# A float32 trunk on split operands: 2x2 block chains without subtracted copies, w_down one block later, left operands made one by one behind weight splits

## The chip, the cores and the metric

One core of a Trainium2 chip runs the whole program. The metric is the time of one execution on the device, in microseconds (us), as the median of three runs. The engines work side by side, each through its own queue in order: TensorE (PE in the rows, PEld its weight loads), VectorE (DVE), ScalarE (ACT), GpSimd (POOL) and SyncE (SP), which issues the loads of weights. An instruction at the head of a queue that waits holds everything behind it.

## The reference

256 positions of width 2048 go through two residual layers, each followed by a SwiGLU layer. The even layer has SSD heads and MLA heads side by side, the odd one stick-breaking attention.

```python
def reference(x, mix_norm, ffn_norm, w_in, ..., w_gate, w_up, w_down, final_norm):
    cos, sin = rope_tables(x.shape[1], x.dtype)
    for layer in range(DEPTH):                       # DEPTH = 2
        h = rms_norm(x, mix_norm[layer])
        if layer % 2 == 0:
            mix = ssd_mla_mixer(h, w_in[e], ..., w_out_even[e], cos, sin)   # concat(y_ssd, y_mla) @ w_out
        else:
            mix = stick_breaking_mixer(h, w_qkv[o], w_out_odd[o])           # heads @ w_out
        x = x + mix
        x = x + swiglu_ffn(rms_norm(x, ffn_norm[layer]), w_gate[layer], w_up[layer], w_down[layer])
    return rms_norm(x, final_norm)

def swiglu_ffn(h, w_gate, w_up, w_down):
    return (jax.nn.silu(h @ w_gate) * (h @ w_up)) @ w_down
```

D_MODEL is 2048, the hidden width of the SwiGLU layer 5632 (11 blocks of 512), everything is float32.

## The kernel before

**Split operands.** Every float32 operand of a matmul is split into a high and a low half: ACT casts it to the high half (L268), DVE subtracts that from the operand to get the low half (L269). A product is then three matmuls: high by high, low by high, high by low. Left operands are transposed on TensorE so that the contraction lies on the partitions.

**A pair.** `pair` multiplies the 256 rows by two blocks of 512 columns of weights at a time (w_gate and w_up of one hidden block; two blocks of an out-projection). Its contraction of 2048 falls in four blocks of 512. Blocks 0 and 1 are done as a 2x2 block product with seven multiplications in place of eight, M1 to M7, whose left operands are seven sums of quarters of x (`st["S"]`) and whose right operands are the weight blocks b11, b12, b21, b22 and four differences of them (t1, t2, b12 in place, M4's). Blocks 2 and 3 are done plainly as c0 to c3, two tiles each. So a pair has 15 products of 12 matmuls (128x512), 11 splits of weights and four weight differences (L526, `wsub`). Raw weights lie in a ring of four 1 MB tiles, high and low halves in rings of three each, differences in a ring of two.

**Banks.** A pair accumulates in four PSUM banks, z, p2, p3 and p4. In the kernel before M1, M5, M6 and M7 all go to z, and after each of them ACT copies the bank out (L612). DVE twice subtracts an earlier copy (L615), so that what is left can be added to the other banks; z itself, when complete, needs no copy. The order of the products is the tuple `MIXED`, or `LATE` in the second half of an out-projection of MLA and of the stick-breaking layer.

**Operands of a pair.** `operand_block` transposes one block of the left side. When the second of blocks 0 and 1 is there, `operand_ready` makes the four sums and seven splits in one go; with `wait` over 1 (15 from `norm_operand`), under a pressing priority and not before the last copy of a product (`self.kept`).

**Order of the work.** TensorE's order is written by hand: tasks (generators for transposes, attention heads and so on) are woken at `tick()`, at most two at a time, between the matmuls of the big products. On the other engines a scheduler sets the order by priority: weight work counts up from 100000 (`wprio`), work under `urgent()` has 50000, anything else 10000000. `issue_after` forbids an instruction to come ahead of another one.

**SwiGLU layer.** Groups of 2, 2, 2, 2 and 3 pairs; after each group the transposed activations of the group are multiplied by the group's rows of w_down, four column blocks one after another, each added to the residual (`xres`, L425).

Other lines that the rows name: L278 transposes a block of x and L289 to L290 make its halves; L304 and L1120 copy transposed tiles out of PSUM; L444 adds a copy of a product to a bank; L474, L497 and L498 make the operand sums of `operand_ready`; L769 is the stick-breaking output product; L1135 and L1159 are the scores and the output of an MLA head, L1155 is the ACT copy ahead of the latter; L361 to L363 are the matmuls of `project` (w_in, w_qkv, w_down), L559 those of `pair`.

## Time and profile before

| | before |
| --- | --- |
| time, median of 3 runs | 2460.2 us (2457.3 to 2462.13) |
| the profiled execution's own time | 2460.24 us |
| its span, first to last instruction | 2458.5 us |
| TensorE busy | 2419.7 us, 98% |
| DVE busy | 1837.9 us, 75% |
| ACT busy | 1344.2 us, 55% |
| chain that ended last, by engine | PE 88%, DVE 7%, issue 2%, ACT 1%, DMA 1% |
| mean granted clock of TensorE | 0.996 |

TensorE is busy for nearly all of the span, and the chain followed back from the end runs over it for 88%. The time is in two parts, then: what TensorE has to do, and the few stretches in which it isn't at work or has a low clock. Those stretches are found by cutting the span in pieces of 50 us, and read in the timelines of the engine that is waited for.

### The profile page before, as it was taken

The page shows a single profiled execution, that of the slowest core. Times are in us where ns is not written, and L with a number is a line of the kernel's source. Part 1 is how long each engine was busy: PE and PEld are TensorE (multiplying, and loading weights), DVE is VectorE, ACT ScalarE, POOL GpSimd, SP SyncE. Part 2 cuts the span into 40 slices and gives each one's busy share as a digit, 9 for nine tenths or more (in the row PEclk, how much of TensorE's full clock was granted, in tenths as well). Part 3 has the DMA queues.
Part 4 walks back from the last instruction along what each step waited for, and adds up shares of the span by engine and source line. Part 5 has one row for each costly group of instructions (what it writes and reads, how often), then busy time and mean ns, then how long its engine had stood idle before and what let it go on. Part 6 is the DMA issues. An engine that isn't in the chain of part 4 may idle for free.

```text
span 2458.5 us, 27627 instructions
## 1 busy us (share of the span) xinstructions
PE 2419.7 (98%) x11104; PEld 1991.0 (81%) x11104; DVE 1837.9 (75%) x1561; ACT 1344.2 (55%) x1337; POOL 136.9 (6%) x165
## 2 busy tenths in 40 slices
PE   8999999999999999999999999999999999999998
PEld 7888888777788888888888888878788888888887
DVE  5876596578988878787975446469988888787975
ACT  6665564455654555454554556656654545454563
POOL 1341101110000000000000000000000000000001
PEclk9999999999999999999999999999999999999999
DMA  8564556424555556565655555545556656565653
GB/s 273 174 204 154 171 189 187 126 98 138 202 208 187 203 179 218 171 234 175 223 189 189 173 171 169 173 137 177 192 196 201 201 185 203 180 229 171 240 193 115
DMA packets 257824, 454.77 MB, mean 185 GB/s; under 512 B 20716, under 2 KB 45424, under 8 KB 257696
## 3 DMA queue, kind: packets, MB, share of 16 engines
q1 hardware_dynamic: 255168, 446.48, 54.3%
q0 software_dynamic: 1952, 5.48, 0.7%
q8 instruction: 87, 1.43, 0.2%
q10 hardware_dynamic: 576, 1.05, 0.1%
q14 instruction: 41, 0.34, 0.0%
HBM read 450.85 MB, written 2.13 MB: 184 GB/s over the span
## 4 chain that ended last, share of the span: by engine, by line
PE 88%; DVE 7%; issue 2%; ACT 1%; DMA 1%; SPq 0%; ACTq 0%; DVEq 0%
PE acc L559 39%; PE acc L361 14%; PE acc L363 14%; PE acc L362 14%; DVE wl L269 4%; PE tr L278 1%; DVE wsum L526 1%; ACT wh L268 1%; PE at L1060 1%; PE at L1136 1%; PE tr L302 0%; DVE w L526 0%; DVE s L269 0%; PE at L1135 0%; DVE s L444 0%
## 5 line engine op out<-in xcount | busy, mean ns | idle before, releaser
L269 DVE TENSOR_TENSOR wl<-w,wh 128x2048 fp32r<-128x2048 f32 (+2 forms) x431 | 967.9, 2256 | 391.3 <-ACT wh L268 387.9
L268 ACT CAST wh<-w 128x2048 fp32r<-128x2048 f32 (+2 forms) x431 | 804.7, 1876 | 537.2 <-PE acc L363 312.7
L559 PE MATMUL acc<-wh,s 128*128 128x512 f32 x3360 | 842.7, 392 | 5.8 <-DVE s L269 2.4
L559 PEld LDWEIGHTS acc<-wh,s 128*128 128x128 f32 x3360 | 628.1, 188 | 137.0 <-ACT s L612 3.6
L361 PE MATMUL acc<-wh,s 128*128 128x512 f32 (+1 forms) x1600 | 637.7, 399 | 0.6 <-ACT wh L268 0.6
L363 PE MATMUL acc<-wh,s 128*128 128x512 f32 (+1 forms) x1600 | 622.1, 389 | 0.0
L362 PE MATMUL acc<-wl,s 128*128 128x512 f32 (+1 forms) x1600 | 620.8, 388 | 0.2 <-DVE wl L269 0.2
L559 PE MATMUL acc<-wl,s 128*128 128x512 f32 x1680 | 453.0, 391 | 6.2 <-DVE wl L269 6.0
L559 PEld LDWEIGHTS acc<-wl,s 128*128 128x128 f32 x1680 | 314.6, 188 | 77.9 <-DVE wl L269 12.9
L363 PEld LDWEIGHTS acc<-wh,s 128*128 128x128 f32 x1600 | 301.0, 188 | 63.4
L362 PEld LDWEIGHTS acc<-wl,s 128*128 128x128 f32 x1600 | 301.8, 189 | 58.0 <-issue 1.2
L361 PEld LDWEIGHTS acc<-wh,s 128*128 128x128 f32 x1600 | 301.7, 189 | 57.7 <-issue 1.2
L269 DVE TENSOR_TENSOR wl<-wsum,wh 128x2048 fp32r<-128x2048 f32 x84 | 192.0, 2297 | 15.1 <-ACT wh L268 15.0
L268 ACT CAST wh<-wsum 128x2048 fp32r<-128x2048 f32 x84 | 160.9, 1915 | 69.1 <-PE acc L559 33.6
L526 DVE TENSOR_TENSOR wsum<-w,wsum 128x2048 f32<-128x2048 f32 x56 | 128.6, 2297 | 9.9 <-DMA w<-in_w_up_dram 7.9
L612 ACT COPY s<-acc 128x512 f32<-128x512 f32 x112 | 65.7, 586 | 103.8 <-PE acc L559 103.8
L629 ACT ACTIVATE s<-s,rstd 128x512 f32<-128x512 f32 x44 | 31.9, 725 | 103.6 <-DVE s L628 103.6
L773 POOL TENSOR_SCALAR_AFFINE_SELECT s<-s 128x256 f32<-128x256 f32 x16 | 15.7, 980 | 1112.2 <-ACT s L772 1112.2
L526 DVE TENSOR_TENSOR wsum<-w,w 128x2048 f32<-128x2048 f32 x28 | 64.7, 2312 | 8.2 <-DMA w<-in_w_up_dram 5.6
L526 DVE TENSOR_TENSOR w<-w,w 128x2048 f32<-128x2048 f32 x28 | 64.4, 2299 | 0.0
L425 DVE TENSOR_TENSOR xres<-acc,xres 128x512 f32<-128x512 f32 x76 | 51.4, 689 | 10.9 <-PE acc L363 10.3
L316 ACT ACTIVATE s<-acc,rstd 128x512 f32<-128x512 f32 x48 | 32.1, 687 | 45.3 <-PE acc L363 44.0
(230 smaller groups left out, 1277.5 us busy)
## 6 DMA issues: line engine op xcount, KB each, us to landing
w<-in_w_gate_dram SPq DMA_DIRECT2D x88, 1024.0 KB, 5.1
w<-in_w_up_dram SPq DMA_DIRECT2D x88, 1024.0 KB, 5.1
w<-in_w_down_dram SPq DMA_DIRECT2D x88, 1024.0 KB, 5.1
w<-in_w_qkv_dram SPq DMA_DIRECT2D x48, 1024.0 KB, 5.1
w<-in_w_in_dram SPq DMA_DIRECT2D x47, 1024.0 KB, 5.1
w<-in_w_out_even_dram SPq DMA_DIRECT2D x32, 1024.0 KB, 5.0
w<-in_w_out_odd_dram SPq DMA_DIRECT2D x16, 1024.0 KB, 4.9
w<-in_w_ukv_dram SPq DMA_DIRECT2D x32, 256.0 KB, 4.2
```

Of the source, the lines that this page charges most:

```text
L268: nc.scalar.copy(hi, src)
L269: nc.vector.tensor_tensor(lo, src, hi.bitcast(F32), op=ALU.subtract)
L278: self.nc.tensor.transpose(pt[:, k, t * P:(t + 1) * P], src(t, 2 * k2 + k), self.ident)
L316: self.nc.scalar.activation(o, ps[t], func, scale=scale[:, t:t + 1])
L361: nc.tensor.matmul(ps[t], hi[:, ts], wh, start=k == 0, stop=False)
L362: nc.tensor.matmul(ps[t], hi[:, ts], wl, start=False, stop=False)
L363: nc.tensor.matmul(ps[t], lo[:, ts], wh, start=False, stop=k == nk - 1)
L425: nc.vector.tensor_tensor(xs, c, xs, op=ALU.add)
L526: self.nc.vector.tensor_tensor(o, p, q, op=ALU.subtract)
L559: nc.tensor.matmul(ps[b], x, y, start=b not in started, stop=stop, skip_group_check=True)
L612: self.kept = [nc.scalar.copy(o, ps["z"]).ins]
L629: nc.scalar.activation(s, s, AF.Silu, scale=rstd[:, t:t + 1])
```

## The change

1. The banks are dealt out anew: M1, M6 and M7 go to z, M5 and M3 to p3, M2 to p2, M4 to p4. The two subtractions of copies (L615) of a pair go, and z, which now has no M5 in it, gets one more addition of a copy. Four copies remain.
2. Two new orders: `HALF` for the SwiGLU layer and the second half of each out-projection, `LATE` for the first half (now that of SSD too). The order of the loads follows. Each weight difference is issued just ahead of the product that needs it, or one or two ahead, not all at the head of the pair.
3. w_down: after each pair from the third on two w_down blocks of the group before are done, so that a group's blocks come one pair later and two by two; the last group of three stays last.
4. `operand_ready` may run as a task of its own (`pace=1`): two steps for the sums, then one operand at a tick, each not ahead of the last weight split so far (`self.last_split`). `norm_operand` waits 9 ticks, not 15; `norm_block` 2 and 6.
5. Tasks carry a priority, given when they are started: transposes of an MLA group and its heads get the pressing one. One task of an SSD group waits 3 ticks, not 1.

The diff, cut to its core (lines of the changed file are 1 to 12 higher than those of before):

```diff
     def advance(self, t):
         try:
-            t["wake"] = self.now + next(t["gen"])
+            with self.priority(t["rank"]):
+                t["wake"] = self.now + next(t["gen"])
...
-                           g[:, 4 * j:4 * j + 4], squares, 15)
+                           g[:, 4 * j:4 * j + 4], squares, 9)
...
         for n in (0, 2):
-            self.pair(st, view(n), view(n + 1), add(n), add(n + 1), self.MIXED if n else order)
+            self.pair(st, view(n), view(n + 1), add(n), add(n + 1), self.HALF if n else self.LATE)
...
             yield wait
-            with ExitStack() as order:
-                if wait > 1:
-                    order.enter_context(self.urgent())
-                    for ins in self.kept:
-                        order.enter_context(self.tc.issue_after(ins))
-                self.operand_ready(st, j, res)
+            self.operand_ready(st, j, res, 1)
...
+        def paced():
+            if not pace:
+                return nullcontext()
+            return self.tc.issue_after(self.last_split)
...
+            for n, a in enumerate((a11, a12, a22, s1, s2, a21, s4)):
+                yield pace
+                hi, lo = self.s2([4, P], F32R), self.s2([4, P], F32R)
+                with paced():
+                    self.split(hi, lo, a)
+                st["S"].append((hi, lo))
+        if pace:
+            st["paced"] = self.spawn(gen())
...
-    MIXED = ("M1", "M3", "M5", "M2", "M6", "M4", "M7", "c0", "c1", "c2", "c3")
-    LATE = ("M1", "M3", "M5", "M2", "M6", "c0", "M4", "M7", "c1", "c2", "c3")
+    HALF = ("M1", "M5", "c0", "M3", "M6", "M2", "M7", "M4", "c1", "c2", "c3")
+    LATE = ("M1", "M5", "M2", "M3", "M6", "M4", "M7", "c0", "c1", "c2", "c3")
...
+        for m in ("b11", "b12", "c0", "b22", "b21", "c1", "c2", "c3") if order is self.HALF else (
+                "b11", "b12", "b22", "b21", "c0", "c1", "c2", "c3"):
...
-        self.wsub(t1, raw["b12"], raw["b11"])
-        w = {"M1": self.wsplit(raw["b11"])}
-        self.wsub(t2, raw["b22"], t1)
-        self.wsub(raw["b12"], raw["b22"], raw["b12"])
...
-        todo = {"z": 6, "p3": 3, "p2": 3, "p4": 3}
+        todo = {"z": 5, "p3": 4, "p2": 3, "p4": 3}
...
+            if keep:
+                with self.urgent():
+                    o = kept[keep] = self.s2([512])
+                    self.kept = nc.scalar.copy(o, ps[b]).ins
...
+        bank = {"M1": "z", "M6": "z", "M7": "z", "M5": "p3", "M3": "p3", "M2": "p2", "M4": "p4"}
...
         for m in order:
+            if m == "M1":
+                self.wsub(t1, b12, b11)
+            if m == order[2]:
+                self.wsub(t2, b22, t1)
+            if m == order[3]:
+                self.wsub(b12, b22, b12)
             if m == "M4":
-                src[m] = self.wsum()
-                self.wsub(src[m], raw["b21"], t2)
...
-            if b == "z":
-                with self.urgent():
-                    o = kept[m] = self.s2([512])
-                    self.kept = [nc.scalar.copy(o, ps["z"]).ins]
-                    for n, q in (("M5", "M1"), ("M7", "M5")):
-                        if m == n:
-                            self.kept.append(nc.vector.tensor_tensor(o, o, kept[q], op=ALU.subtract).ins)
...
-        for nb in (2, 2, 2, 2, 3):
...
+        act, held = [], []
+        for n in range(HID // 512):
+            act.append(gate_up(n))
+            for c in held[:2]:
+                down(*c)
+            held = held[2:]
+            if len(act) == 2 and n < 8:
+                held = [(act, n - 1, c) for c in range(4)]
+                act = []
...
-            self.norm_block(st, n, g, rank=self.URGENT)
+            self.norm_block(st, n, g, 2 if n == 2 else 6, self.URGENT)
...
-        yield 1
+        yield 3
...
-        tasks = [self.spawn(self.mla_head(h, qp, q, k, v, g, o, 2 + 4 * h, done)) for h in range(4)]
+        tasks = [self.spawn(self.mla_head(h, qp, q, k, v, g, o, 2 + 4 * h, done), self.URGENT) for h in range(4)]
```

What this does to the queues stands at three places. DVE, last group of the stick-breaking layer (s2<-tr is the copy of transposed weights that L769 waits for, wl a low half of weights, wsum and w the differences t2 and b12), before:

```order
L304 COPY s2_2035_11840<-tr_2034_11835 128x512
L269 TENSOR_TENSOR wl_2066_11980<-w_2064_11977,wh_2065_11979 128x2048
L526 TENSOR_TENSOR wsum_2084_12040<-w_2077_12027,wsum_2083_12039 128x2048
L526 TENSOR_TENSOR w_2076_12025<-w_2077_12027,w_2076_12025 128x2048
L304 COPY s2_2040_11859<-tr_2039_11854 128x512
```

and with the change, where the second copy stands ahead of both differences:

```order
L305 COPY s2_2035_11825<-tr_2034_11820 128x512
L270 TENSOR_TENSOR wl_2066_11965<-w_2064_11962,wh_2065_11964 128x2048
L305 COPY s2_2040_11844<-tr_2039_11839 128x512
L538 TENSOR_TENSOR wsum_2084_12025<-w_2077_12012,wsum_2083_12024 128x2048
L538 TENSOR_TENSOR w_2076_12010<-w_2077_12012,w_2076_12010 128x2048
```

DVE, end of the second MLA out-projection pair and head of the SwiGLU layer (the last row is c3's low half; L269 on s2 are low halves of left operands, L497 their sums, L526 differences of the next pair), before:

```order
L269 TENSOR_TENSOR s2_953_5087<-s2_919_4915,s2_952_5086 128x512
L269 TENSOR_TENSOR s2_955_5091<-s2_928_4943,s2_954_5090 128x512
L526 TENSOR_TENSOR wsum_978_5217<-w_971_5203,w_970_5201 128x2048
L269 TENSOR_TENSOR s2_957_5095<-s2_947_5075,s2_956_5094 128x512
L269 TENSOR_TENSOR s2_959_5099<-s2_948_5076,s2_958_5098 128x512
L526 TENSOR_TENSOR wsum_979_5218<-w_972_5205,wsum_978_5217 128x2048
L444 TENSOR_TENSOR s2_920_4917<-acc_914_4889,s2_920_4917 128x512
L269 TENSOR_TENSOR s2_961_5103<-s2_924_4932,s2_960_5102 128x512
L425 TENSOR_TENSOR xres_80<-s2_920_4917,xres_80 128x512
L269 TENSOR_TENSOR s2_963_5107<-s2_949_5077,s2_962_5106 128x512
L444 TENSOR_TENSOR s2_944_5044<-acc_915_4890,s2_944_5044 128x512
L269 TENSOR_TENSOR wl_969_5171<-w_907_4876,wh_968_5170 128x2048
```

and with the change; c3's low half is the seventh row, and t1's difference and the residual's additions (L444, L430) stand behind it, as t2's does further on:

```order
L270 TENSOR_TENSOR wl_961_5098<-w_905_4869,wh_960_5097 128x2048
L270 TENSOR_TENSOR s2_949_5054<-s2_919_4910,s2_948_5053 128x512
L270 TENSOR_TENSOR s2_951_5066<-s2_928_4938,s2_950_5065 128x512
L270 TENSOR_TENSOR s2_957_5082<-s2_938_5016,s2_956_5081 128x512
L270 TENSOR_TENSOR wl_967_5134<-w_906_4871,wh_966_5133 128x2048
L270 TENSOR_TENSOR s2_959_5094<-s2_939_5017,s2_958_5093 128x512
L270 TENSOR_TENSOR wl_969_5166<-w_907_4873,wh_968_5165 128x2048
L270 TENSOR_TENSOR s2_963_5106<-s2_924_4927,s2_962_5105 128x512
L538 TENSOR_TENSOR wsum_978_5213<-w_971_5199,w_970_5197 128x2048
L444 TENSOR_TENSOR s2_920_4912<-acc_912_4879,s2_920_4912 128x512
L270 TENSOR_TENSOR s2_965_5118<-s2_940_5018,s2_964_5117 128x512
```

ACT in the first MLA group, where TensorE waits for the copy of s2<-tr (L1155, now L1166), before:

```order
L739 COPY s2_647_3745<-at_769_4257 128x128
L268 CAST s2_773_4269<-s2_577_3442 128x512
L268 CAST s2_775_4273<-s2_646_3744 128x512
L268 CAST s2_777_4277<-s2_647_3745 128x512
L268 CAST s2_779_4281<-s2_770_4262 128x512
L268 CAST s2_781_4285<-s2_771_4263 128x512
L268 CAST s2_783_4289<-s2_578_3443 128x512
L268 CAST s2_785_4293<-s2_772_4264 128x512
L1155 COPY s2_788_4301<-tr_787_4297 128x384
```

and with the change, where one cast of weights stands ahead of it and the operand's casts come behind it, not in a row:

```order
L269 CAST wh_836_4465<-w_816_4430 128x2048
L1166 COPY s2_774_4269<-tr_773_4265 128x384
L1156 ACTIVATE s2_778_4286,sm_777_4285<-at_775_4277,mx_776_4284 128x128
L1156 ACTIVATE s2_778_4286,sm_777_4285<-at_775_4277,mx_776_4284 128x256
L269 CAST s2_781_4310<-s2_577_3440 128x512
L269 CAST s2_785_4327<-s2_646_3742 128x512
L315 COPY s2_787_4331<-acc_764_4238 128x512
```

## Rows read from the trace of the kernel before

**Rows 1.** The page: busy time of each engine, its share of the span, instructions.

```profile
PE 2419.7 (98%) x11104; PEld 1991.0 (81%) x11104; DVE 1837.9 (75%) x1561; ACT 1344.2 (55%) x1337; POOL 136.9 (6%) x165
```

**Rows 2.** Stretches of 50 us: busy time (and instructions), TensorE's granted clock, DMA share, GB/s.

```profile
550.00:600.00 50.00, 45.43 (x213) 35.44 (x212) 38.48 (x43) 25.42 (x33) 0.00 (x0) 1.00 0.44 148
600.00:650.00 50.00, 46.74 (x210) 38.41 (x209) 49.79 (x43) 31.58 (x37) 0.00 (x0) 0.97 0.49 168
900.00:950.00 50.00, 50.00 (x226) 41.41 (x225) 45.31 (x29) 30.90 (x23) 0.00 (x0) 1.00 0.56 189
1600.00:1650.00 50.00, 46.07 (x207) 37.78 (x207) 27.65 (x20) 25.05 (x31) 4.24 (x4) 0.97 0.44 147
1700.00:1750.00 50.00, 46.41 (x201) 37.80 (x200) 47.64 (x41) 29.30 (x32) 0.00 (x0) 0.93 0.47 168
```

**Rows 3.** Timeline of TensorE, steady part: start, duration, engine, line, operation, [idle before <-releaser].

```profile
1030.39 1.98 PE L559 MATMUL acc<-wh,s 128*128 128x512 f32 x8
...
1033.11 1.98 PE L559 MATMUL acc<-wh,s 128*128 128x512 f32 x8
```

**Rows 4.** Waits of TensorE: line waited for, us in total, times, longest.

```profile
PE acc L559 <- DVE wl L269: 6.0, 7, 3.1
PE at L769 <- DVE s L304: 3.9, 2, 3.3
...
PE at L1159 <- ACT s L1155: 2.8, 3, 1.4
...
PE tr L278 <- DVE xres L425: 2.5, 2, 2.0
PE acc L559 <- DVE s L269: 2.4, 1, 2.4
PE acc L559 <- ACT s L612: 1.8, 3, 0.7
PE acc L559 <- ACT wh L268: 1.4, 1, 1.4
PE at L1135 <- DVE s L1120: 1.3, 1, 1.3
```

**Rows 5.** The page, costliest groups: busy, mean ns of one | idle before, releaser.

```profile
L269 DVE TENSOR_TENSOR wl<-w,wh 128x2048 fp32r<-128x2048 f32 (+2 forms) x431 | 967.9, 2256 | 391.3 <-ACT wh L268 387.9
...
L268 ACT CAST wh<-wsum 128x2048 fp32r<-128x2048 f32 x84 | 160.9, 1915 | 69.1 <-PE acc L559 33.6
L526 DVE TENSOR_TENSOR wsum<-w,wsum 128x2048 f32<-128x2048 f32 x56 | 128.6, 2297 | 9.9 <-DMA w<-in_w_up_dram 7.9
L612 ACT COPY s<-acc 128x512 f32<-128x512 f32 x112 | 65.7, 586 | 103.8 <-PE acc L559 103.8
```

**Rows 6.** Timeline of DVE and of TensorE, last group of the stick-breaking layer.

```profile
1628.79 2.49 DVE L526 TENSOR_TENSOR wsum<-w,wsum 128x2048 f32<-128x2048 f32 x1
...
1633.62 0.68 DVE L304 COPY s<-tr 128x512 f32<-128x512 f32 x1
...
1634.35 0.70 PE L769 MATMUL at<-s,s 128*128 128x256 f32 x2 [3.28 <-DVE s L304]
```

**Rows 7.** Timeline of DVE and of TensorE, second MLA out-projection pair and after it.

```profile
595.36 0.69 DVE L444 TENSOR_TENSOR s<-acc,s 128x512 f32<-128x512 f32 x1 [1.22 <-PE acc L559]
...
633.24 2.28 DVE L269 TENSOR_TENSOR wl<-w,wh 128x2048 fp32r<-128x2048 f32 x1
...
644.67 0.63 PE L278 MATMUL tr<-ident,xres 128*128 128x128 f32 x4 [1.97 <-DVE xres L425]
```

**Rows 8.** Timeline of TensorE, second out-projection pair of the stick-breaking layer.

```profile
1738.76 2.07 PE L559 MATMUL acc<-wl,s 128*128 128x512 f32 x4 [3.09 <-DVE wl L269]
...
1744.05 1.38 PE L559 MATMUL acc<-wl,s 128*128 128x512 f32 x4
```

**Rows 9.** Timeline of ACT, first MLA group.

```profile
519.46 1.82 ACT L268 CAST s<-s 128x512 fp32r<-128x512 f32 x3 [0.44 <-DVE s L497]
```

**Rows 10.** Timeline of DVE, first MLA out-projection pair.

```profile
582.60 2.28 DVE L526 TENSOR_TENSOR w<-w,w 128x2048 f32<-128x2048 f32 x1
```

More of the change, by code (lines that the diff above doesn't have):

```diff
@@ L82, in after_urgent, with spawn @@
         return order
[L85 to L87 removed]
+    def spawn(self, gen, rank=None):
+        t = {"gen": gen, "wake": self.now, "done": False, "rank": rank or self.tc.cur_priority}
         self.tasks.append(t)
@@ L379, in project, with operand_tile @@
         return ps
+    def operand_tile(self, st, k, t):
+        return tuple(o[:, t * P:(t + 1) * P] for o in self.pairs(st["xT"])(k))
     def pairs(self, blocks):
@@ L560, in mm, with add @@
             started.add(b)
-        def product(b, s, w):
-            (hi, lo), (wh, wl) = st["S"][s], w
-            for k in range(4):
-                mm(b, hi[:, k], wh[:, k])
-                mm(b, lo[:, k], wh[:, k])
-                if k == 1:
-                    self.tick()
-            for k in range(4):
-                mm(b, hi[:, k], wl[:, k], stop=k == 3)
-            self.tick()
-        def tile(b, k0, w):
+        def add(b, x, w, keep=None):
             wh, wl = w
-            ts = slice(0, P) if b in ("p2", "p3") else slice(P, S)
-            ops = [[o[:, ts] for o in xT(k0 + k)] for k in range(4)]
-            for k, (hi, lo) in enumerate(ops):
+            n = len(x)
+            for k, (hi, lo) in enumerate(x):
@@ L589, in finish @@
             with self.urgent():
-                for b, q, take, t in (("p2", "M1", left, 0), ("p4", "M7", left, 1), ("z", None, right, 1),
+                for c, q, take, t in (("p2", "M1", left, 0), ("p4", "M7", left, 1), ("z", "M5", right, 1),
                                       ("p3", "M6", right, 0)):
-                    if todo[b] == 0 and (q is None or q in kept):
-                        todo[b] = -1
-                        take(t, ps[b], kept.get(q))
-        for m in order:
+                    if todo[c] == 0 and q in kept:
+                        todo[c] = -1
+                        take(t, ps[c], kept[q])
@@ new lines, in pair @@
+        bank = {"M1": "z", "M6": "z", "M7": "z", "M5": "p3", "M3": "p3", "M2": "p2", "M4": "p4"}
+        place = {"M1": 0, "M2": 1, "M4": 2, "M5": 3, "M6": 4, "M7": 5, "M3": 6}
+        ops = lambda m: [(st["S"][place[m]][0][:, k], st["S"][place[m]][1][:, k]) for k in range(4)]
+        for m in order:
+            if m == "M1":
[4 more added lines that the diff above has]
+                self.wsub(b12, b22, b12)
@@ L616, in pair @@
-            finish()
+            add(bank[m], ops(m), w, m if m in ("M1", "M5", "M6", "M7") else None)
     def ffn(self, layer, st, gain_next):
@@ L632, in right @@
         def right(t, c, s):
-            if s is not None:
-                nc.vector.tensor_tensor(s, c, s, op=ALU.add)
-                c = s
-            nc.vector.scalar_tensor_tensor(h[t], c, rstd[:, t:t + 1], h[t], op0=ALU.mult, op1=ALU.mult)
-        n0 = 0
-        for nb in (2, 2, 2, 2, 3):
-            act = []
-            for n in range(n0, n0 + nb):
-                self.pair(st, self.cols(wg, n * 512), self.cols(wu, n * 512), left, right)
-                res = []
-                act.append((self.spawn(self.transpose_split(
-                    lambda t, k, h=tuple(h): h[t][:, k * P:(k + 1) * P], res, rank=self.URGENT)), res))
-            aT = self.pairs(act)
-            last = n0 + nb == HID // 512
-            nst = self.norm_begin() if last else None
-            for n in range(4):
-                view = self.cols(wd, n * 512, r0=n0 * 512)
-                if last and gain_next is None:
-                    self.final(n, aT, view, 4 * nb)
-                    continue
-                ps = self.project(aT, view, 4 * nb)
-                self.add_residual(ps, n)
-                if last:
-                    self.norm_block(nst, n, gain_next)
-            n0 += nb
@@ new lines, in right, with gate_up, down @@
+            nc.vector.tensor_tensor(s, c, s, op=ALU.add)
+            nc.vector.scalar_tensor_tensor(h[t], s, rstd[:, t:t + 1], h[t], op0=ALU.mult, op1=ALU.mult)
+        def gate_up(n):
+            self.pair(st, self.cols(wg, n * 512), self.cols(wu, n * 512), left, right)
+            res = []
+            return self.spawn(self.transpose_split(
+                lambda t, k, h=tuple(h): h[t][:, k * P:(k + 1) * P], res, rank=self.URGENT)), res
+        def down(act, n0, n):
+            ps = self.project(self.pairs(act), self.cols(wd, n * 512, r0=n0 * 512), 4 * len(act))
+            self.add_residual(ps, n)
@@ new lines, in ffn @@
+        act, held = [], []
[7 more added lines that the diff above has]
+                act = []
+        nst = self.norm_begin()
+        for n in range(4):
+            if gain_next is None:
+                self.final(n, self.pairs(act), self.cols(wd, n * 512, r0=8 * 512), 12)
+                continue
+            down(act, 8, n)
+            self.norm_block(nst, n, gain_next)
```

92 lines of the change are left out of this document (46 added, 46 removed).

## The prediction

> **What bounds the kernel now.** I read the page first: TensorE is busy for 2419.7 us of the span of 2458.5 [rows 1]. In a stretch of 50 us from the middle of a feed-forward layer, 900 to 950, it is busy for all 50.00 at a granted clock of 1.00 [rows 2]. There the twelve matmuls of one product follow each other in 2.72 us (1030.39 to 1033.11) [rows 3], 0.227 us for a matmul. The change neither adds nor removes matmuls (in both programs 9636 rows stand in TensorE's order), so only time in which TensorE stands or runs slowly can be won or lost. I read the waits of TensorE next [rows 4]. They name its stalls: 6.0 us for low halves of weights in 7 waits, 3.9 for the copy of transposed stick weights, 2.8 for ACT's copy L1155, 2.5 for a residual that is about to be transposed, 2.4 for low halves of a left operand, 1.8 for copies of products, 1.4 for one cast, 1.3 for L1120: 22.1 us in 20 waits, all outside the steady part. An idle time begins where a matmul's modelled end lies, 0.39 us after its start, though the next could start after 0.227. So each wait costs 0.16 us more than it shows: 20 x 0.16 = 3.2. And after long waits the clock is low: 0.97 of full speed in the mean of the stretches 600 to 650 and 1600 to 1650, 0.93 in 1700 to 1750 [rows 2].
>
> Prices [rows 5]: a low half of weights 2.26 us on DVE, a weight difference 2.30; on ACT a cast of weight sums 1.92 and a copy of a product 0.59. A small DVE operation of 128x512 takes 0.69 [rows 6, 7].
>
> **The change, part by part.** The time is made against the profiled execution, 2460.24 us (1.74 more than its span), practically the median of 2460.2.
>
> (1) *Last group of the stick-breaking layer.* DVE does two weight differences from 1628.79 and only at 1633.62 the copy of 0.68 us for which TensorE waits 3.28 us [rows 6]. The program now has that copy ahead of both. Two starts lie 2.4 us apart, so the copy comes 4.8 us earlier and the wait goes. The other wait for L304 (3.9 - 3.28 = 0.6) remains: the instruction ahead of that copy is unchanged. After the wait the mean clock of 0.97 in the 50 us is worth 0.03 x 50 = 1.5 us. Gain 3.28 + 0.16 + 1.5 = 4.9.
>
> (2) *From the second out-projection pair into the feed-forward layer, twice.* In the even layer DVE works through from 595.36 until c3's low half, begun at 633.24: 37.88 us [rows 7], 8 low halves, 3 weight differences and 22 small operations. TensorE runs dry at c3, and 1.97 us again at 644.67, where the residual's addition (L425) stands behind a difference and a low half. Now 8 low halves, 1 difference and 15 small ones stand between the same addition and c3's low half. By the prices that is 2 x 2.30 + 7 x 0.69 = 9.4 us less: c3's low half, for which TensorE had run dry by then, comes some 9 us earlier. The work hasn't vanished: only the two L615 subtractions go; t2's and b12's differences come in the next pair, and additions follow c3. What is late next is c0, now third in the order, whose operands are block 2 of the residual: addition, transposes and low half have to be ready two products (5.4 us) after the pair's start, with t2's difference among them. Walking DVE's new order by these durations I get them 1.0 to 1.4 us late; I leave 1.2. In the odd layer the same order of work gives the wait of 3.09 us at 1738.76, and the next twelve matmuls take 5.29 us (to 1744.05) in place of 2.72 [rows 8]. There I leave 2.0, since w_up's blocks landed later. Here lie the 6.0 us of waits for low halves and the 2.5 for the residual [rows 4]; nine waits add 9 x 0.16 = 1.4; clock 0.93 costs 0.07 x 50 = 3.5, and 0.97 in the even layer 1.5. Together 14.9, of which 3.2 remain: gain 11.7.
>
> (3) *ACT in the last SSD and MLA groups.* Seven casts of operands stand in a row ahead of L1155; the last three of them run 1.82 us from 519.46 [rows 9], and TensorE waits for L1155, 1.4 us at the longest [rows 4]. Operands now come one by one behind weight splits and L1155 stands right behind one weight cast. The wait for L1120 (1.3) has the matching row of subtractions on DVE as its cause. Gain 1.4 + 1.3 + 0.3 = 3.0; the same casts are still done, between later weight casts, where ACT is busy 55% [rows 1].
>
> (4) *First MLA out-projection pair.* TensorE waits 2.4 us for the last head's low halves [rows 4], behind differences of weights, the last of which DVE begins at 582.60 [rows 10]. Only t1 and one low half now stand ahead of them. With the L612 copies (1.8), the remaining 1.4 of L1155 and 6 x 0.16 this pair loses 6.6 us. Walking the new order I find 3 to 4 left, most of it a new wait of L1166 (the former L1155) behind a cast. I take a gain of 3.0; bounds 0 and 6.6.
>
> (5) *SSD out-projection.* M4's cast waited for its difference; DVE now does that difference ahead of the low halves of M2 and M7. Gain 1.4 + 0.16 = 1.6.
>
> (6) *Each of the 28 pairs.* Two subtractions go and one addition of 0.69 comes: 0.69 us less of DVE, worth nothing where TensorE is busy 50.00 of 50 and DVE 45.31 [rows 2]. The copy of M7 now has one product (2.72 us) before c1 writes the same bank; before, c0 gave it 5.44 more. If a cast of 1.92 has just begun, cast and copy end after 2.51, so 0.2 us are spare and I cost it at nothing. M4's difference, cast and low half are a chain of 2.30 + 1.92 + 2.26 = 6.5 us; in pairs 0 to 2 (and 10) of each feed-forward layer it follows M7's low half directly. TensorE has M7's last four matmuls and M4's first eight (2.72) to cover it, so it needs DVE 3.8 us ahead at M7; my walk gives 3.7 to 5. Cost 0.16 in eight pairs, 1.3; bounds 0 and 8 x 3.8 = 30. The two w_down blocks between later pairs give DVE time, and there M4's difference stands well ahead. w_down one block later leaves the count of loads and the tail as they were.
>
> Sum: 4.9 + 11.7 + 3.0 + 3.0 + 1.6 - 1.3 = 22.9, so 2460.2 - 22.9 = 2437 us. If every stall named here went, it would be 2460.2 - (4.9 + 14.9 + 3.0 + 6.6 + 1.6) = 2429; some waits too short for the list could add 3 to that.
>
> **Rivals.** *The stall moves.* The head of each feed-forward layer keeps a wait of about 2 us for block 2's operands and the slow matmuls behind it, and the MLA pair gains nothing: 11.7 halves to 6, 3.0 to 0, and the sum is 14: 2446. For it: the new third place of c0, and a wait of 1.97 us, after which the clock of 600 to 650 was 0.97. Against: the 9 us by which DVE is ahead.
>
> *M7's copy is late.* With 0.5 us lost in 28 pairs, 14 us come back: 2451. For it: L612 already stopped TensorE 3 times [rows 4]. Against: all of them were in the MLA pair, where softmax work shares ACT.
>
> *No gain at all.* The paced operands become the new end of each out-projection, and what is taken from the weight splits is waited for at M1: all of (2) and (4) stays and the sum is 9.5 - 1.3 = 8 at best, and less with the copy: 2452 to 2460.
>
> *Slower.* M4's chain finds DVE without a lead in the eight pairs of (6): 3.8 us each, 30 us, against 24.2 of the other terms: 2466. It decides from 24.2 / 8 = 3.0 us a pair, that is, a lead under 0.8. For it: three pairs follow each other with no w_down between them, and 45.31 of 50 us are DVE work. Against: DVE had 4.69 idle in that stretch.
>
> *Clock.* In 550 to 600, where TensorE was busy for only 45.43 of 50 us and waited up to 2.4 us at a time, the clock stayed at 1.00, and so it did in the steady stretch, whose products go through four banks [rows 2, 4]. So a short wait at a bank costs its own length. The Trainium skill says otherwise: "TensorE: Matmul & The Clock Gate", section "A second HAM failure mode: psum-queue depth-cycling", has a kernel whose short idles between groups, while cycling through PSUM banks, made the clock swing between its two levels. Were new short waits at the banks to do that here in 22 pairs, each would cost what 1738.76 shows, 5.29 - 2.72 = 2.57 us, 57 us in all: 2494. No stretch of this trace shows it, so it gets 0.02.
>
> **How the numbers follow.** The forecast, 2426 to 2444, 0.52; the stall moves, 0.20; late copy, 0.07; no gain, 0.10, of which I put 0.03 below the bound of faster; M4's chain, 0.09; clock, 0.02. A measurement can tell 0.2%, 4.9 us, from no change, so faster means below 2455.3: 0.52 + 0.20 + 0.07 + 0.03 = 0.82; the same 0.07; slower 0.11. The range runs from 2426 to 2456: it takes in the forecast, the moved stall and the late copy.
>
> **What would show it.** The list of waits should lose L304's 3.3 us, the wait for the residual, and L1135's; the waits for low halves should fall from 6.0 to about 2. Stretches 600 to 650 and 1700 to 1750 should have clock 1.00, and DVE should reach c3's low half some 9 us earlier against TensorE. Steady stretches should keep 50.00 of 50. I am wrong if the first three pairs of a feed-forward layer show waits for M4's low half, if copies of M7 stop TensorE at c1, or if c0 of the first pair waits over 2 us with a clock below 1.00 behind it.

## The result and the profile after

Measured side by side, the changed kernel takes 2446.7 us (2442.86 to 2448.24) and the one before 2459.8: a ratio of 0.9946, 95% interval 0.9933 to 0.9959, so 13.1 us less. The forecast was 2437. The sign and the range hold; of the 22.9 us that the sum gave, a little over half arrived.

The page, TensorE's busy time, which answers to [rows 1]:

```profile
PE 2412.8 (99%) x11104; PEld 1989.3 (81%) x11104; DVE 1818.8 (74%) x1533; ACT 1345.5 (55%) x1337; POOL 136.3 (6%) x165
```

The waits of TensorE after the change, which answer to [rows 4] (line waited for, us in total, times, longest); L576 is the former L559, L269 the former L268, L270 the former L269, L305 the former L304, L430 the former L425, L779 the former L769, L1146 and L1170 the former L1135 and L1159; L290 makes the low half of a transposed block of x, L470 transposes a block of the residual, L996 is a SiLU on ACT in the SSD groups and L1054 their transposes:

```profile
PE acc L576 <- ACT wh L269: 4.5, 3, 2.2
PE acc L576 <- DVE wl L270: 3.8, 6, 1.1
...
PE acc L576 <- DVE s L290: 2.6, 2, 1.8
PE tr L1054 <- ACT s L996: 1.9, 1, 1.9
PE at L1170 <- ACT s L1166: 1.5, 1, 1.5
PE tr L470 <- DVE xres L430: 1.2, 1, 1.2
PE at L1146 <- DVE s L305: 0.7, 1, 0.7
```

Gone are the waits for the last head's low halves (2.4), for the stick copy (3.9), for copies of products (1.8) and the long ones for low halves of weights (6.0 with one of 3.1, now 3.8 with none over 1.1). Others have come: 4.5 us for casts of weights, 2.6 for L290, 1.9 for a SiLU of the SSD groups. The rows of [rows 4] that the prediction added up held 22.1 us in 20 waits, these hold 16.2 in 15. Stretches of 50 us, as in [rows 2]:

```profile
100.00:150.00 50.00, 48.12 (x228) 39.08 (x227) 35.10 (x62) 30.87 (x34) 20.14 (x19) 0.97 0.52 165
600.00:650.00 50.00, 49.17 (x225) 40.47 (x224) 48.20 (x44) 34.73 (x39) 0.00 (x0) 1.00 0.57 189
900.00:950.00 50.00, 50.00 (x222) 41.43 (x221) 39.75 (x22) 25.51 (x18) 0.00 (x0) 1.00 0.58 197
1600.00:1650.00 50.00, 47.59 (x220) 39.28 (x219) 32.20 (x25) 31.28 (x39) 5.49 (x4) 1.00 0.38 126
1700.00:1750.00 50.00, 48.21 (x220) 39.32 (x219) 50.00 (x46) 34.51 (x41) 0.00 (x0) 1.00 0.54 179
```

In the three stretches that had clocks of 0.97, 0.97 and 0.93 it is 1.00, which by the prediction's own measure is 6.5 us. In 100 to 150, where nothing was expected, it is now 0.97. The steady stretch is as full as before, 50.00 of 50. That DVE has 39.75 us there where it had 45.31 is mostly a matter of which work now falls into the stretch: over the whole span DVE has 19.1 us less, 28 operations of about 0.69, one for each pair. Put together, 5.9 us of waits, 5 x 0.16 = 0.8 under them, 6.5 and less 1.5 for the clock are 11.7 of the 14.2 between the spans (2458.5 and 2444.3 us); the rest lies in waits that these rows don't hold. That is the account of one execution of each kernel; the clock was not the same in all of them (last section).

Two of the places, looked at closely. In the last group of the stick-breaking layer the copy now stands ahead of both differences (timeline of DVE, for [rows 6]); behind it a cast of weights is late, since ACT does L806 first, which waits for L805 on DVE, which stands behind M4's difference (DVE, ACT, TensorE):

```profile
1621.28 0.68 DVE L305 COPY s<-tr 128x512 f32<-128x512 f32 x1
1621.88 2.28 DVE L538 TENSOR_TENSOR wsum<-w,wsum 128x2048 f32<-128x2048 f32 x1
...
1641.32 2.28 DVE L538 TENSOR_TENSOR wsum<-w,wsum 128x2048 f32<-128x2048 f32 x1
...
1644.10 0.52 ACT L806 ACTIVATE s<-s 128x384 f32<-128x384 f32 x1 [2.21 <-DVE s L805]
1644.53 1.88 ACT L269 CAST wh<-w 128x2048 fp32r<-128x2048 f32 x1
...
1646.47 2.11 PE L576 MATMUL acc<-wh,s 128*128 128x512 f32 x8 [2.20 <-ACT wh L269]
```

In the first pair of the feed-forward layer M4's difference, cast and low half are one chain behind M7's low half (DVE, ACT, DVE), and TensorE waits for it twice (DVE, ACT, TensorE):

```profile
653.50 2.28 DVE L270 TENSOR_TENSOR wl<-w,wh 128x2048 fp32r<-128x2048 f32 x1
...
655.94 2.27 DVE L538 TENSOR_TENSOR wsum<-w,wsum 128x2048 f32<-128x2048 f32 x1
...
660.23 2.29 DVE L270 TENSOR_TENSOR wl<-wsum,wh 128x2048 fp32r<-128x2048 f32 x1 [1.36 <-ACT wh L269]
...
658.30 1.90 ACT L269 CAST wh<-wsum 128x2048 fp32r<-128x2048 f32 x1 [2.48 <-DVE rstd L258]
...
658.05 1.07 PE L576 MATMUL acc<-wl,s 128*128 128x512 f32 x4
660.25 2.11 PE L576 MATMUL acc<-wh,s 128*128 128x512 f32 x8 [1.14 <-ACT wh L269]
662.58 1.19 PE L576 MATMUL acc<-wl,s 128*128 128x512 f32 x4 [0.22 <-DVE wl L270]
```

### The profile page after: what moved, and what is told of

It reads as the page before. It is cut to its first block, busy times and chain, and to the rows that moved or that the text cites. A ratio compares the mean times of both kernels' runs of the same rounds, so it can differ in the third digit from the quotient of the medians.

```text
span 2444.3 us, 27566 instructions
## 1 busy us (share of the span) xinstructions
PE 2412.8 (99%) x11104; PEld 1989.3 (81%) x11104; DVE 1818.8 (74%) x1533; ACT 1345.5 (55%) x1337; POOL 136.3 (6%) x165
## 5 line engine op out<-in xcount | busy, mean ns | idle before, releaser
L270 DVE TENSOR_TENSOR wl<-w,wh 128x2048 fp32r<-128x2048 f32 (+2 forms) x431 | 967.3, 2255 | 355.2 <-ACT wh L269 352.1
L269 ACT CAST wh<-w 128x2048 fp32r<-128x2048 f32 (+2 forms) x431 | 804.9, 1876 | 479.1 <-PE acc L364 246.5
L576 PE MATMUL acc<-wh,s 128*128 128x512 f32 x3360 | 838.5, 391 | 7.1 <-ACT wh L269 4.5
L576 PEld LDWEIGHTS acc<-wh,s 128*128 128x128 f32 x3360 | 627.5, 188 | 137.7 <-ACT wh L269 5.5
L576 PE MATMUL acc<-wl,s 128*128 128x512 f32 x1680 | 450.8, 390 | 3.9 <-DVE wl L270 3.8
L576 PEld LDWEIGHTS acc<-wl,s 128*128 128x128 f32 x1680 | 314.7, 188 | 73.3 <-DVE wl L270 8.4
L270 DVE TENSOR_TENSOR wl<-wsum,wh 128x2048 fp32r<-128x2048 f32 x84 | 192.0, 2287 | 42.8 <-ACT wh L269 42.7
L269 ACT CAST wh<-wsum 128x2048 fp32r<-128x2048 f32 x84 | 160.6, 1915 | 93.0 <-PE acc L364 60.6
L595 ACT COPY s<-acc 128x512 f32<-128x512 f32 x112 | 65.7, 587 | 96.6 <-PE acc L576 96.6
L269 ACT CAST s<-tr 128x512 fp32r<-128x512 f32 x44 | 25.8, 587 | 87.8 <-PE tr L279 87.8
```

The source lines that it names most:

```text
L269: nc.scalar.copy(hi, src)
L270: return nc.vector.tensor_tensor(lo, src, hi.bitcast(F32), op=ALU.subtract).ins
L576: nc.tensor.matmul(ps[b], x, y, start=b not in started, stop=stop, skip_group_check=True)
L595: self.kept = nc.scalar.copy(o, ps[b]).ins
```

## The experiments

Each run was timed in five rounds beside the kernel before on the same chip, so the ratios compare, not the times alone.

| run | time, us | ratio to before, interval |
| --- | --- | --- |
| changed kernel | 2446.7 | 0.9946 [0.9933, 0.9959] |
| e1 differences at the head | 2446.3 | 0.9949 [0.9937, 0.9961] |
| e2 operands in one go | 2445.9 | 0.9946 [0.9934, 0.9958] |
| e3 priority only where named | 2445.1 | 0.9945 [0.9933, 0.9956] |
| e4 M4's difference earlier | 2444.2 | 0.9941 [0.9929, 0.9953] |
| e5 no task priorities | 2469.2 | 1.0037 [1.0025, 1.0050] |
| e6 e1 and e2 together | 2447.3 | 0.9947 [0.9935, 0.9960] |
| e7 banks and orders only | 2466.6 | 1.0029 [1.0020, 1.0038] |
| e8 w_down as before | 2452.0 | 0.9969 [0.9958, 0.9981] |
| e9 before, ordinary work presses | 2451.6 | 0.9967 [0.9955, 0.9980] |
| e10 priority ends with its task | 2462.7 | 1.0010 [1.0001, 1.0019] |
| e11 three amendments | 2446.4 | 0.9941 [0.9928, 0.9953] |
| e12 two amendments | 2441.8 | 0.9923 [0.9909, 0.9937] |

**Late differences or paced operands?** The prediction's explanation was that less DVE work stands ahead of what TensorE waits for, because differences come late and operands one by one. e1 undoes the first:

```diff
+        self.wsub(t1, b12, b11)
+        first = self.wsplit(b11)
+        self.wsub(t2, b22, t1)
+        self.wsub(b12, b22, b12)
...
-            if m == "M1":
-                self.wsub(t1, b12, b11)
-            if m == order[2]:
-                self.wsub(t2, b22, t1)
-            if m == order[3]:
-                self.wsub(b12, b22, b12)
```

> The changed kernel with the differences t1, t2 and b12 issued at the head of each pair again, as before; everything else as changed. Theory A (late differences carry most of the gain): the copy of transposed stick weights comes behind two differences again, so TensorE waits about 3.3 us there and runs some 1.5 us slow behind it, c3's low half of the second out-projection pairs comes 4.6 us later, and the MLA pair waits some 2.4 us more: 8 to 12 us longer than the changed kernel, 2455 to 2459 us. Theory B (the paced operands carry it): the waits stay as in the changed kernel, 2446 to 2449 us.

e2 undoes the second (and the two other calls of `operand_ready` likewise):

```diff
-            self.operand_ready(st, j, res, 1)
+            with ExitStack() as order:
+                if wait > 1:
+                    order.enter_context(self.urgent())
+                    order.enter_context(self.tc.issue_after(self.kept))
+                self.operand_ready(st, j, res)
```

> The changed kernel with operand_ready in one go again, with its former priority and place; everything else as changed. Theory A (late differences carry most of the gain): only the first MLA group's two waits of 1.4 and 1.3 us come back, with c3's low half late by less than 1 us: 2449 to 2451 us. Theory B (the paced operands carry it): the seven casts and subtractions stand ahead of c3's low half in both layers again, waits of 1.3 and 3.1 us with low clock behind them, and the MLA group's waits: 10 us longer than the changed kernel, 2457 us.

e6 is both together:

> The changed kernel with the differences at the head of each pair again and operand_ready in one go again. Theory A (each of the two takes enough work out of DVE's way, so that undoing one alone did not show): now c3's low half of the second out-projection pairs is late again, by 1.3 us in the even and 3 us in the odd layer, with low clock behind it: 5 to 8 us longer than the changed kernel, 2451 to 2455 us. Rival (neither matters, the new order of the products made the room): 2445 to 2448 us.

All three take the changed kernel's time within the intervals, in a kernel that keeps the task priorities. In e1 the stick copy isn't late even with the differences at the head. Low halves of weights are waited for 4.8 us longer, casts 2.3 less, and the 2.6 us for c0's operands (L290) are gone from the list, so it comes out even. The two rows of its waits (L580 is the changed kernel's L576):

```profile
PE acc L580 <- DVE wl L270: 8.6, 6, 3.7
...
PE acc L580 <- ACT wh L269: 2.2, 1, 2.2
```

So neither carries the gain, alone or with the other. The explanation fell.

**The tasks' priorities.** e3 leaves a task its own priority only where the spawn names one (the MLA transposes and heads); e5 takes that away too, since its spawn records no rank for any task. The line that both share:

```diff
-            with self.priority(t["rank"]):
+            with self.priority(t["rank"]) if t["ranked"] else nullcontext():
```

> The changed kernel in which a task has a priority of its own only where the spawn names one; the others run at the priority of the moment, as before. Theory A (the new wait of 1.9 us at 110 us, before which ACT loads tables for the SSD group's exponentials between two SiLUs, comes from the priority that each task now keeps from its start): the wait and the low clock behind it go, 3.5 us less than the changed kernel, about 2443 us. Rival (it comes from the longer wait of three ticks ahead of those transposes): the wait at 110 stays, 2446 to 2448 us.

> The changed kernel in which no task carries a priority, neither its own from the start nor the pressing one of the MLA transposes and heads; differences late and operands paced as changed. In its order the copy of transposed stick weights stands behind two differences again, as before. Theory A (the pressing priority carries the gain of the MLA groups and, by way of the order that the scheduler then finds, that of the stick copy): waits of 3.3 us with 1.6 of low clock come back in the last stick group and 2 to 3 us in the MLA group and its out-projection, while the 3.5 us at 110 us go: 2449 to 2452 us. Rival (late differences and paced operands carry the gain): those waits stay away and only the 3.5 us go, 2443 us.

e3's wait at 110 us goes, and the clock of 100 to 150 is 1.00 again, but by the medians only 1.6 us of it arrive, and by the ratios 0.2, which the intervals don't tell from nothing. e5 is 22 us slower than the changed kernel, where Theory A gave 2 to 5. The waits of TensorE in e5, low halves of left operands (L270) and the stick copy:

```profile
PE acc L576 <- DVE s L270: 21.5, 3, 8.3
PE at L779 <- DVE s L305: 3.3, 1, 3.3
```

Of the 21.5 us in three waits, two lie at the heads of the feed-forward layers, far behind the last MLA task. Why a priority of MLA tasks reaches there the code tells. `priority` sets the scheduler's priority, yields and puts the former one back, without `try` and `finally`. A task that ends raises `StopIteration` through it, and the line that puts the priority back is skipped. The priorities noted while the changed program is built bear it out: from the 318th of its 1640 ticks to the end, what ran at 10000000 and more runs at 50000 and some, ahead of all weight work at 100000 and more. e10 puts the priority back:

```diff
         keep, self.tc.cur_priority = self.tc.cur_priority, at
-        yield
-        self.tc.cur_priority = keep
+        try:
+            yield
+        finally:
+            self.tc.cur_priority = keep
```

> The changed kernel with the former priority put back also where a task ends, so that only the MLA transposes and heads themselves press and all ordinary work behind them has the priority behind weights again. Theory A (what counts is the ordinary work, not the MLA tasks): paced operands stand behind weight splits again, with one wait of 7 to 8 us at the head of each feed-forward layer and 3.3 us in the last stick group; only the MLA waits of 6 us in the run without task priorities stay away: 2463 to 2470 us. Rival (the pressing MLA tasks are what counts): 2445 to 2450 us.

Theory A holds: 2462.7 us, at the lower edge of what it gave, and the gain is gone. The waits of e10, and its head of the feed-forward layer (DVE, then TensorE): the paced operands' low halves come only when DVE has done differences and low halves of weights (L272 is the former L269, L540 the former L526).

```profile
PE acc L578 <- DVE s L272: 14.5, 2, 7.2
PE at L781 <- DVE s L307: 3.3, 1, 3.3
```

```profile
642.47 2.28 DVE L540 TENSOR_TENSOR wsum<-w,wsum 128x2048 f32<-128x2048 f32 x1
644.68 2.49 DVE L272 TENSOR_TENSOR s<-s,s 128x512 fp32r<-128x512 f32 x4
...
645.41 1.65 PE L578 MATMUL acc<-wh,s 128*128 128x512 f32 x3 [7.24 <-DVE s L272]
```

e9 gives the kernel before that priority and nothing else:

```diff
+        if g == 0:
+            self.tc.cur_priority = self.URGENT + 10
```

> The kernel before with one line more: from the first MLA group on, ordinary work (whatever has no priority of its own) has the pressing priority, ahead of weight splits, as it has in the changed kernel once a task with that priority has ended. Banks, orders, differences, operands and w_down as before. Theory A (this priority is what carries the gain): the waits of 3.3 us for the stick copy, of 2.4 us for low halves of left operands and of 2 us for the residual go, 8 to 15 us less than before, 2445 to 2452 us. Rival (the priority only mends what the new orders and the paced operands would spoil): the same as before within 4 us.

It is 9.2 us faster than before by this one line, within what Theory A gave. In its waits the stick copy no longer appears, nor does a wait of 2.4 us for low halves of left operands; low halves of weights, the residual and the copies of products remain. By the ratios the rest of the change is worth some 5 us more where this priority is on (0.9967 to 0.9946, the intervals touch) and costs 2 us where it is off (e10, 1.0010). The changed kernel with its former w_down (e8, below) has nearly the ratio of e9, 0.9969: beside the priority only the later w_down adds, and the other parts together add nothing.

```profile
PE acc L559 <- DVE wl L269: 5.4, 6, 3.2
PE tr L278 <- DVE xres L425: 3.4, 2, 2.0
...
PE acc L559 <- ACT s L612: 3.0, 4, 1.2
```

**Banks, orders and w_down.** e7 is the kernel before with the new `pair`, differences at its head; e8 the changed kernel with the former grouping:

> The kernel before with the new banks and product orders and the loads that follow them, and nothing else of the change: differences at the head, operands in one go, w_down after each group, the former waits, no task priorities. Theory A (the two subtractions a pair are worth nothing, since TensorE does not wait in the steady part, and c0 in third place costs 1 to 2 us at the head of each feed-forward layer): 2458 to 2462 us. Rival (banks and orders carry the gain): 2446 to 2449 us.

```diff
-            for c in held[:2]:
-                down(*c)
-            held = held[2:]
             if len(act) == 2 and n < 8:
-                held = [(act, n - 1, c) for c in range(4)]
+                for c in range(4):
+                    down(act, n - 1, c)
                 act = []
```

> The changed kernel with the former grouping of w_down: four blocks right after each second pair. Theory A (a later w_down moves no wait of TensorE but the 0.19 us for M4's low half in pairs 1 and 2): 2446 to 2447 us, and no wait in the steady part. Rival (with the groups' activations needed right after the pair, their transposes and low halves are waited for): 0.5 to 1 us in each of eight groups, 2450 to 2454 us.

e7 is 7 us slower than before, worse than Theory A. In e8 the rival holds. The waits in which both differ from the kernel before, transposes of the activations (L279) behind the last multiplication of a pair (e7, then e8):

```profile
PE tr L279 <- DVE s L643: 4.5, 8, 1.2
```

```profile
PE tr L279 <- DVE s L641: 3.9, 5, 1.0
```

When w_down follows its pair at once, the transposes need h right away, and in the new banks z needs an addition and a multiplication at the end where it had a multiplication. In the changed kernel a pair stands between. By the ratios, 0.9969 to 0.9946, the later w_down is worth 5 to 6 us, though the intervals touch. Whether the addition alone makes the wait, or also the order of the loads, was not separated. e7 has other waits that add to its 7 us: 5.9 us for low halves of left operands in the MLA pair, where the kernel before has 2.4, and 2.6 us for the residual at the head of each feed-forward layer, where it has 2.0 and 0.5. (In both kernels `LATE` is the order of the first pair of an out-projection, not of its second half.)

**Amendments.** e4 issues M4's difference one product earlier:

```diff
-            if m == "M4":
+            if m == order[order.index("M4") - 1]:
```

> The changed kernel with M4's difference issued one product earlier. Theory A (in the first pair of each feed-forward layer M4's difference, cast and low half are one chain that nothing covers, 1.3 us for the cast and 0.4 for the low half, and 0.19 in the next two): these waits go, 3 to 4 us less than the changed kernel, 2443 us. Rival (DVE and ACT are late there with everything, and the difference only changes places with M7's low half): M7's low half is late instead, by about the same, 2446 to 2448 us.

e11 adds e3's edit to it and moves c0 to the sixth place, its load to the fifth; e12 is e3's and e4's edits alone:

> The changed kernel with three amendments: a task has its own priority only where one is named, M4's difference comes one product earlier, and c0 stands sixth in the order of the products with its load fifth. Theory A (each removes its own wait: 3.5 us in the SSD groups, 3.3 in the first pairs of the feed-forward layers, 3 us at c0): 9 us less than the changed kernel, 2437 to 2440 us. Rival (DVE has as much to do at the head of a feed-forward layer as before, and the wait at c0 moves to the next low half): 2441 to 2444 us.

> The changed kernel with two amendments: a task has its own priority only where one is named, and M4's difference comes one product earlier; c0 third, as changed. Theory A (the two waits stand in different stages and go independently: 3.5 us at 110 us, of which the run with the first alone gave 1.6 back as shorter waits elsewhere, and 2 us in the first pairs): 3 to 5 us less than the changed kernel, 2442 to 2444 us. Rival (as with three amendments, what is taken away comes back at another low half): 2446 us.

In e4 the casts lose 2.3 of their 4.5 us of waits, and low halves 1.7 of 3.8; by the ratios that is 1.2 us, inside the intervals. e11 gains nothing over the changed kernel: c0's wait is gone, and in its place stand new ones for low halves and for the residual (L470). e12 takes 2441.8 us, the fastest of all, 18.8 under the 2460.6 of the kernel before beside it; its interval and the changed kernel's still touch (0.9937 and 0.9933). Waits of e11, then of e12:

```profile
PE acc L575 <- DVE wl L270: 6.7, 6, 2.0
PE tr L470 <- DVE xres L430: 4.3, 2, 2.8
```

```profile
PE acc L576 <- DVE s L290: 2.9, 2, 1.8
...
PE acc L576 <- ACT wh L269: 2.6, 1, 2.6
PE acc L576 <- DVE wl L270: 1.8, 2, 1.0
```

## Why the prediction was right in sign and too high in gain

*What bounds the kernel* held: the steady stretches did not move but for one wait, and nearly all that was won or lost lies in the stretches that the waits named, and in one that they did not. The one wait is 1.02 us for a low half of weights at 2144.84, in a stretch that was full before; DVE had waited 2.53 us for a w_up load at 2132.49. Added up as the prediction adds (each wait with 0.16 us, the clock by stretches), the two traces give for its terms:

| term | forecast, us | the two traces, us |
| --- | --- | --- |
| (1) last stick group | 4.9 | 3.0 |
| (2) into the feed-forward layers | 11.7 | 10.3 |
| (3) last SSD and MLA groups | 3.0 | 2.1 |
| (4) first MLA out-projection pair | 3.0 | 3.8 |
| (5) SSD out-projection | 1.6 | 0.7 |
| (6) M4's chain | -1.3 | -3.4 |
| SSD groups | none | -3.5 |
| the wait at 2144.84 | none | -1.2 |
| sum | 22.9 | 11.8 |

In (1) 1.5 us and in (2) 5.0 are clock; they hold for the profiled executions.

*(1)* The stick copy's wait and the low clock went as told. The walk covered DVE and not ACT: a cast stands behind L806 there, 2.20 us of new wait at 1646.47 and 0.22 behind it. With 0.16 under each that is 2.7 us, more than half of the 4.9. The other wait for the copy, 0.65 us, which was to remain, went too.

*(2)* The size left for c0 was right: 2.6 us of waits for L290 in the list, 1.8 the longest, against 1.2 and 2.0. In the profiled execution clock 1.00 in both stretches also came as forecast. A wait of 1.2 us for the residual (L470 at 594.79) is new. In the even layer c3's low half is ready at 624.43, 6.2 us before TensorE turns to it, where it had come 1.28 late: 7.5 us earlier, not 9. The reason given for the gain was not. e1, e2 and e6 take away what I counted (differences and operands) and keep the time; e9 and e10 show what moved the work, ordinary operations that go ahead of weight splits. I had read where each row stood in the new order, so the terms came out near, but not what put it there: that they did is luck, since nothing in the prediction counted on a priority left on.

*(3)* Of the wait of L1135 (now L1146), 1.3 us, 0.7 remain, for another copy (L305); L1159's 1.45 is gone. *(4)* The wait of L1170 behind a cast that the walk found is there with 1.5 us, and 1.02 for a low half at 548.40 is new; the gain of 3.8 is near the 3.0 that I took. Of the 1.8 us for copies of products 0.7 lay in the first out-projection pair of the stick-breaking layer (1680.02), not in the MLA pair; so the argument against the late copy, that all three waits were in the MLA pair, was misread.

*(5)* The 1.4 us for M4's cast went, but 1.11 us for a low half came at 333.16, in the same out-projection. It is a size of DVE that I had not looked for, told in the last section.

*(6)* M4's chain was the mis-sized term. I gave 0.16 us to eight pairs alike, 1.3 in all, because my walk found DVE 3.7 us or more ahead. In the first pair of each layer it was not: 1.14 us for the cast and 0.22 for the low half, 0.32 more with what the list leaves under each wait, in both layers. DVE was ahead by 2.3 us there, not 3.7: M7's low half ends at 655.78 and TensorE uses it at 658.05. A wait for M4's low half was one of the signs of being wrong that the prediction named. Two subtractions a pair were worth nothing in the steady part, as told, but the addition that I costed at nothing, and w_down one block later, which I costed at nothing, belong together: without the latter, 5 to 6 us come back.

*Not seen at all:* the SSD groups. A task keeps the priority of its start, so the group's decay work goes ahead of the convolution on DVE, and ACT changes tables three times where it did once in that place (timeline of ACT after):

```profile
96.46 1.28 ACT L1045 ACT_TABLE_LOAD   x1
...
107.49 1.28 ACT L996 ACT_TABLE_LOAD   x1 [2.81 <-DVE s L994]
...
111.76 1.28 ACT L1045 ACT_TABLE_LOAD   x1
```

The transposes L1054 wait 1.9 us, and the clock of 100 to 150 is 0.97, together some 3.5 us; in e3, without these priorities, both are gone. I had read the new order from the out-projections on, and not where the trace of before had no wait.

The forecast that the stall moves gave 2446 us, which is the time measured, but not for its reason: block 2's operands took what I had left for them, the clock stayed at 1.00, and the MLA pair did gain. The late copy did not occur: no wait for L595 is in the list. Nor did the swinging clock occur: with waits of 0.2 to 2.2 us at the products, every stretch of 50 us up to 2400 has 1.00 but the one of the SSD groups, and in e7 and e8, with eight and five waits of 0.3 to 1.2 us behind pairs, the stretches of the feed-forward layers in which they lie have 1.00 too. The rule that stood beside that rival (the Trainium skill, TensorE: Matmul & The Clock Gate, section "A second HAM failure mode: psum-queue depth-cycling") did not show itself here.

What stays open: why e3's 3.5 us gave 0 to 2. The traces of e3 and e12 show single waits of 0.5 to 0.8 us at other pairs, where DVE waited for a w_up load, and 2.6 in place of 2.2 us for the cast behind L806. That e12's edits seem to give more together than each alone may be no more than the clock: executions with the same mean clock of 0.997 take 2447.4 to 2448.2 us in the changed kernel (three), 2446.4 and 2446.7 in e3, 2444.4 in e4 (median of five) and 2443.4 in e12 (one), so some 1.5, 3.5 and 4.5 us less, as far as a clock rounded to 0.001 lets one tell.

## What to carry to other kernels

A row that stands elsewhere in the new order gives the size of a gain, but its reason has to be looked for in what gives it its place; here a priority that was never put back carried it, which one line in the kernel before (e9) and one in the changed kernel (e10) settled. Walk each engine's queue of the changed program through every stage, those without a wait before above all: the three terms that were missing stood on queues that the walk had left out. A part that is costed at nothing may still hold another up: with the new banks and without the later w_down, 5 to 6 us come back. And before a difference of two traces is put down to an edit, look at the clock of the other executions.

## What the runs showed of the hardware

**One wait, two clocks.** In the last stick group TensorE waits 2.6 us for the same cast in e3 and in e12. Behind it the same eight matmuls take 2.10 us in e3, at a granted clock of 1.00, and 3.78 in e12, at 0.50 from 1642 to 1648 and 0.79 to 1650, 3.4 us lost (timelines of TensorE, e3, then e12):

```profile
1646.41 2.10 PE L576 MATMUL acc<-wh,s 128*128 128x512 f32 x8 [2.63 <-ACT wh L269]
```

```profile
1642.75 3.78 PE L576 MATMUL acc<-wh,s 128*128 128x512 f32 x8 [2.64 <-ACT wh L269]
```

In the same way the wait of 1.8 us for L290 in the odd layer has 1.00 behind it in the changed kernel and half the clock in e4 and e12: in 1738 to 1742 the mean is 0.57 in e4, which costs 0.43 x 4 = 1.7 us. So a wait of about 2 us may cost its own length or 1.7 to 3.4 us more; which of the two comes, no row here tells. The six executions of the changed kernel bear it out: three have a mean clock of 0.997 and take 2447.4 to 2448.2 us, two have 0.999 and take 2442.9 and 2443.2. The profiled one has 0.998, so the 6.5 us of clock are not won in each. At an equal 0.997 the kernel before takes 2459.0 us (median of the 19 such executions beside the experiments), 11 us more: the greater part of the gain is not clock.

**DVE and GpSimd.** A weight difference or a low half of weights takes DVE 2.28 us by itself. In the SSD out-projection one of each took 3.27 and 3.37 us (timeline of the changed kernel: DVE, GpSimd, and ACT, which squares what GpSimd has multiplied):

```profile
324.21 2.28 DVE L270 TENSOR_TENSOR wl<-wsum,wh 128x2048 fp32r<-128x2048 f32 x1
326.53 3.27 DVE L538 TENSOR_TENSOR wsum<-w,wsum 128x2048 f32<-128x2048 f32 x1
329.73 3.37 DVE L270 TENSOR_TENSOR wl<-w,wh 128x2048 fp32r<-128x2048 f32 x1
...
324.98 5.97 POOL L852 TENSOR_TENSOR s<-s,s 128x512 f32<-128x512 f32 x2 [14.87 <-ACT s L317]
...
327.69 0.63 ACT L265 ACTIVATE s<-s 128x512 f32<-128x512 f32 x1 [0.31 <-POOL s L852]
...
330.99 0.63 ACT L265 ACTIVATE s<-s 128x512 f32<-128x512 f32 x1 [2.57 <-POOL s L852]
```

The rows read as if DVE and GpSimd took turns, each for a whole instruction. The low half of 324.21 has its usual time though GpSimd's first multiplication begins under it; that one ends by 327.69, where ACT takes its result, and the difference, begun at 326.53, is late by about a microsecond. The second ends by 330.99, and the low half begun at 329.73 ends at 333.10, a full 2.1 us after that. TensorE waited 1.11 us for it. In the kernel before, a low half at 324.97 took 3.29 us beside the same work, and nothing waited for it. The Trainium skill (SBUF — State Buffer, section "SBUF: two separate sides") states an exclusive lock on a pair of ports, held for the whole instruction, between a GpSimd operation that reads SBUF and a DVE operation with two inputs in SBUF; the trace agrees, 3.27 and 3.37 us in place of 2.28.
